# Matrix products of two widths in one kernel: in turn, or sixteen of one and then sixteen of the other

## The chip, the cores and the metric

The kernel runs on one core of a Trainium2 chip. The metric is the device time of one execution in microseconds (us); lower is better. Every number below is from one core.

## What is computed

One layer of a hybrid encoder block on 256 positions of 2048 channels, all in float32:

```
u    = rmsnorm(h) * g1
proj = u @ w_in                      # 2048 -> 1024 + 3 * 1024
y_f  = fourier_mix(proj[:, :1024])   # 2-D DFT per channel group, then a linear map
y_a  = dilated_attention(q, k, v)    # 8 heads of 128, three (window, dilation) pairs, ALiBi
h    = h + concat(y_f, y_a) @ w_out  # 2048 -> 2048
u    = rmsnorm(h) * g2
h    = h + relu(u @ w_up) ** 2 @ w_down   # 2048 -> 8192 -> 2048
out  = rmsnorm(h) * g3
```

The weights are some 190 MB, read once; nearly all of the arithmetic is in the products with `w_in`, `w_out`, `w_up` and `w_down`.

## The kernel before

**Two parts per number.** TensorE multiplies a shortened float32 (`F32R`). Every operand x is therefore split into `hi`, its shortened form, which ScalarE writes (line 130), and `lo` = x - hi, which VectorE writes (line 131). A product of two operands is the sum hi·hi + hi·lo + lo·hi, gathered in PSUM.

**Chunks.** The weights come in 1 MB chunks of 128 x 2048 in an order fixed by `_order`. `load_next` has SyncE fetch a chunk into `w_raw`, ScalarE cast it to `w_hi` and VectorE subtract to `w_lo`, the last two in two halves of 1024 columns each. Each of the three tiles has three buffers, and `chunk` keeps two chunks loaded ahead. So the cast of a chunk waits until the products that read the buffer's former `w_hi`, three chunks earlier, are done, and the subtraction waits for those that read the former `w_lo`.

**Strips** (`strip`) make an output of 256 x 512: the activations are the stationary operand, and 512 columns of weights stream. A chunk gives 2 x 4 x 3 = 24 products of 512 columns (`mm3`, lines 138 to 140), and a strip has four chunks: 96 products. `w_out`, `w_down` and the Fourier and v parts of `w_in` are done so.

**Columns** (`column`) make an output of 128 channels x 256 positions, already transposed for what follows: the weights are the stationary operand, and the activations stream. A row of the tile `u` holds the 256 columns of u_hi and then the 256 of u_lo. For each of the 16 slices of 128 channels of the input there is

- a **wide** product (line 237): w_hi against all 512 columns, into all of the PSUM tile `acc`;
- a **narrow** product (line 238): w_lo against the 256 columns of u_hi, added to the second half of `acc`.

`total` (lines 245, 246) then adds the two halves: ScalarE copies one out of PSUM (its COPY), VectorE adds the other. There are 80 columns: 16 for q and k of the eight heads, and 4 x 16 for `w_up`, each group of 16 followed by the four strips of its `w_down` part. (The first column of the MLP takes its own way through `need`.)

**Work in between.** `later` keeps a list of generators and `part` advances each by a step. A column calls `part` after its products 7 and 15. The heads use this: the scores q·k (narrow products into an `aux` tile), a softmax on VectorE and ScalarE, four transposes of the probabilities (line 476), the products with v (narrow too), each a set number of parts after the former. The instruction streams of the engines are made by a scheduler from this program and are executed in order on each engine.

Lines named below: 130 and 131 the split, 138 to 140 `mm3`, 237 and 238 the column, 245 and 246 `total`, 444 the scaling of q and k, 476 the transposes.

Of the kernel before, what the change touches and what calls it, by code (L numbers as in the profile page):

```python
# [20 lines left out]
KT = D // P  # L21
# [11 lines left out]
FIRST = (4, 4, 2, 2, 2)  # L33
WARM = 9
FEW = 224


def _order():
# [30 lines left out]
def tile_block(ctx: ExitStack, tc: tile.TileContext, gx_t, x, w_all, w_f, g_fin,  # L69
# [9 lines left out]
    def acc():  # L79
        return ps_acc.tile([P, NS], F32, name="acc")  # L80
# [18 lines left out]

    few = const.tile([P, FEW], F32, name="few")  # L100
    few_at = [0]

    def small(n, *shape):
        at = few_at[0]
        few_at[0] += n
        assert few_at[0] <= FEW
        t = few[:, at:at + n]
# [70 lines left out]
    def chunk():  # L178
        i = at[0]
        at[0] += 1  # L180
        while len(loaded) < min(i + 1 + AHEAD, len(order)):
            load_next()
        t = loaded[i]
        loaded[i] = None
        return t
# [8 lines left out]
    def part():  # L194
        for gen in list(queue):
            if next(gen, queue) is queue:
                queue.remove(gen)

    def finish():
        while queue:  # L200
            part()
# [23 lines left out]
                part()  # L225
        return ps

    def column(r, parts=(KT // 2 - 1, KT - 1), need=None):

        ps = acc()
        hi, lo = chunk()
        for kt in range(KT):
            if kt == need:
                finish()
            nc.tensor.matmul(ps, hi[:, kt, :], r[:, kt, :], start=kt == 0, stop=False)  # L237
            nc.tensor.matmul(ps[:, S:], lo[:, kt, :], r[:, kt, :S], start=False, stop=kt == KT - 1)  # L238
            if kt in parts:
                part()  # L240
        return ps[:, :S], ps[:, S:]

    def total(ps, pool):
# [244 lines left out]
    for a in range(2):  # L488
        if a:
            ps_v = strip(u_hi, u_lo)  # L490
        v = values(ps_v)
        for hd in range(a * 4, a * 4 + 4):
            q = channels(column(u), "qt", inv_q)
            k = channels(column(u), "kt", inv_k)
            later(head(hd, q, k, v, (2, 3, 2) if hd < NH - 1 else (2, 3, 1)))
# [53 lines left out]
    for gi in range(NGRP):  # L549
        pool = acts if gi % 2 else mlp  # L550
        hidden = [pool.tile([P, KT, S], F32R, name=f"y_{s}") for s in ("hi", "lo")]
        for j in range(KT):
            if gi == 0 and j == 0:
                ps = column(u2, parts=(4, 6, 8), need=KT - CK)
                inv2 = inverse(sums(ss2, "n2"), "n2")
                nc.vector.tensor_copy(out=inv_u, in_=across(inv2, lambda: mlp.tile([P, S], F32, name="relu", bufs=2)[:, :P]))
            else:
                ps = column(u2)
            up(ps, hidden, j)
        for n in range(NN):  # L560
            final = gi == NGRP - 1
            if final and n == NN - 1:
                break
            ps = strip(*hidden)
            ns = slice(n * NS, (n + 1) * NS)
            for m in range(NM):
                hs = h[m][:, ns]
                nc.vector.tensor_add(out=hs, in0=hs, in1=ps[m])  # L568
                if final:
                    squares(ss3, m, n)  # L570
                    nc.vector.tensor_mul(out=hs, in0=hs, in1=g_b[:, ns])
# [121 lines left out]
```

## Time and profile before

| | |
|---|---|
| three runs | 1030.74, 1031.51, 1031.53 us (median 1031.51) |
| the profiled execution | 1031.32 us |
| its span, first to last instruction | 1029.5 us |
| mean granted TensorE clock | 0.999 of full speed |
| TensorE busy (its matmuls) | 1020.2 us, 99% |
| VectorE, ScalarE busy | 610.0 us (59%), 502.8 us (49%) |
| DMA | 195.10 MB, mean 189 GB/s |

The profile names engines PE (TensorE's products), PEld (its loads of the stationary operand, each before its product, beside the product that runs), DVE (VectorE), ACT (ScalarE) and SP (SyncE). The duration given for a product is longer than the distance from its start to the next one's start, because products overlap in the pipeline; so what a product costs is read from the distances between starts, not from the durations or from the busy share.

### The profile page before, as it was taken

The page shows a single profiled execution, that of the slowest core. Times are in us where ns is not written, and L with a number is a line of the kernel's source. Part 1 is how long each engine was busy: PE and PEld are TensorE (multiplying, and loading weights), DVE is VectorE, ACT ScalarE, POOL GpSimd, SP SyncE. Part 2 cuts the span into 40 slices and gives each one's busy share as a digit, 9 for nine tenths or more (in the row PEclk, how much of TensorE's full clock was granted, in tenths as well). Part 3 has the DMA queues.
Part 4 walks back from the last instruction along what each step waited for, and adds up shares of the span by engine and source line. Part 5 has one row for each costly group of instructions (what it writes and reads, how often), then busy time and mean ns, then how long its engine had stood idle before and what let it go on. Part 6 is the DMA issues. An engine that isn't in the chain of part 4 may idle for free.

```text
span 1029.5 us, 12994 instructions
## 1 busy us (share of the span) xinstructions
PE 1020.2 (99%) x5254; PEld 868.3 (84%) x5254; DVE 610.0 (59%) x846; ACT 502.8 (49%) x741; POOL 1.3 (0%) x10
## 2 busy tenths in 40 slices
PE   9999999999999999999999999999999999999997
PEld 7888888888888888888888888888888888888886
DVE  6975775775456656445656545556554546565553
ACT  7754554554446555333555533355543335554441
POOL 0000000000000000000000000000000000000000
PEclk9999999999999999999999999999999999999999
DMA  8653645444555555555554555555555555555542
GB/s 320 233 225 115 263 169 192 156 180 164 189 220 184 184 193 177 202 199 179 195 185 183 202 180 191 204 178 190 187 183 203 198 180 195 180 189 201 180 152 82
DMA packets 32683, 195.10 MB, mean 189 GB/s; under 512 B 3568, under 2 KB 6128, under 8 KB 10608
## 3 DMA queue, kind: packets, MB, share of 16 engines
q1 hardware_dynamic: 32624, 194.28, 53.1%
q8 instruction: 41, 0.67, 0.2%
q14 instruction: 18, 0.15, 0.0%
HBM read 192.17 MB, written 2.10 MB: 189 GB/s over the span
## 4 chain that ended last, share of the span: by engine, by line
PE 97%; DMA 1%; SPq 0%; DVE 0%; ACT 0%; issue 0%; ACTq 0%
PE acc L237 29%; PE acc L139 16%; PE acc L140 16%; PE acc L138 16%; PE acc L238 15%; PE aux L138 1%; PE aux L140 1%; PE aux L139 1%; DMA w_raw<-w_all 1%; SPq L92 0%; PE aux L521 0%; PE aux L476 0%; DVE w_lo L131 0%; ACT w_hi L130 0%; ACT gh L616 0%
## 5 line engine op out<-in xcount | busy, mean ns | idle before, releaser
L131 DVE TENSOR_TENSOR w_lo<-w_raw,w_hi 128x1024 fp32r<-128x1024 f32 (+1 forms) x356 | 423.7, 1209 | 283.2 <-ACT w_hi L130 283.0
L130 ACT CAST w_hi<-w_raw 128x1024 fp32r<-128x1024 f32 (+1 forms) x356 | 362.1, 1041 | 312.6 <-PE acc L140 223.8
L237 PE MATMUL acc<-u,w_hi 128*128 128x512 f32 x1280 | 453.7, 399 | 0.0
L238 PE MATMUL acc<-u,w_lo 128*128 128x256 f32 x1280 | 359.6, 281 | 0.0
L237 PEld LDWEIGHTS acc<-u,w_hi 128*128 128x128 f32 x1280 | 240.6, 188 | 59.0
L138 PE MATMUL acc<-w_hi,y_hi 128*128 128x512 f32 x624 | 243.7, 391 | 0.0
L140 PE MATMUL acc<-w_hi,y_lo 128*128 128x512 f32 x624 | 242.9, 389 | 0.0
L139 PE MATMUL acc<-w_lo,y_hi 128*128 128x512 f32 x624 | 242.9, 389 | 0.0
L238 PEld LDWEIGHTS acc<-u,w_lo 128*128 128x128 f32 x1280 | 241.8, 189 | 0.2
L140 PEld LDWEIGHTS acc<-w_hi,y_lo 128*128 128x128 f32 x624 | 117.1, 188 | 24.6
L138 PEld LDWEIGHTS acc<-w_hi,y_hi 128*128 128x128 f32 x624 | 117.1, 188 | 24.1
L139 PEld LDWEIGHTS acc<-w_lo,y_hi 128*128 128x128 f32 x624 | 117.2, 188 | 23.7
L545 ACT ACTIVATE sq<-relu 128x256 f32<-128x256 f32 x64 | 26.7, 418 | 118.8 <-DVE relu L543 118.8
L131 DVE TENSOR_TENSOR y_lo<-sq,y_hi 128x256 fp32r<-128x256 f32 x64 | 27.2, 425 | 58.0 <-ACT y_hi L130 58.0
L139 PE MATMUL acc<-w_lo,u 128*128 128x512 f32 x120 | 47.2, 394 | 0.5 <-DVE w_lo L131 0.5
L140 PE MATMUL acc<-w_hi,u 128*128 128x512 f32 x120 | 46.8, 390 | 0.0
L138 PE MATMUL acc<-w_hi,u 128*128 128x512 f32 x120 | 46.6, 395 | 0.1
L246 DVE TENSOR_TENSOR total<-acc,total 128x256 f32<-128x256 f32 x80 | 33.4, 418 | 2.6 <-ACT total L245 2.6
L245 ACT COPY total<-acc 128x256 f32<-128x256 f32 x80 | 29.3, 366 | 8.0 <-PE acc L238 8.0
L568 DVE TENSOR_TENSOR gh<-gh,acc 128x512 f32<-128x512 f32 x30 | 20.5, 684 | 16.8 <-PE acc L140 16.8
L139 PEld LDWEIGHTS acc<-w_lo,u 128*128 128x128 f32 x120 | 22.6, 188 | 5.6 <-DVE w_lo L131 1.6
L130 ACT CAST y_hi<-sq 128x256 fp32r<-128x256 f32 x64 | 26.0, 406 | 2.0
(141 smaller groups left out, 474.3 us busy)
## 6 DMA issues: line engine op xcount, KB each, us to landing
w_raw<-w_all SPq DMA_DIRECT2D x171, 1024.0 KB, 4.7
w_raw<-w_all SPq DMA_DIRECT2D x6, 512.0 KB, 7.8
w_raw<-w_all SPq DMA_DIRECT2D x8, 256.0 KB, 5.0
gh<-x SPq DMA_DIRECT2D x8, 256.0 KB, 6.4
out<-gh SPq DMA_DIRECT2D x6, 256.0 KB, 2.4
gh<-gx_t SPq DMA_DIRECT2D x4, 256.0 KB, 6.1
wf<-w_f SPq DMA_DIRECT2D x4, 256.0 KB, 5.0
g_b<-g_fin SPq DMA_DIRECT2D x1, 1024.0 KB, 4.6
```

The costliest lines, as they stand in the source:

```text
L130: nc.scalar.copy(out=hi, in_=src)
L131: nc.vector.tensor_tensor(out=lo, in0=src, in1=f32(hi), op=ALU.subtract)
L138: nc.tensor.matmul(ps, l_hi, r_hi, start=first, stop=False)
L139: nc.tensor.matmul(ps, l_hi, r_lo, start=False, stop=False)
L140: nc.tensor.matmul(ps, l_lo, r_hi, start=False, stop=last)
L237: nc.tensor.matmul(ps, hi[:, kt, :], r[:, kt, :], start=kt == 0, stop=False)
L238: nc.tensor.matmul(ps[:, S:], lo[:, kt, :], r[:, kt, :S], start=False, stop=kt == KT - 1)
L245: nc.scalar.copy(out=t, in_=ps[1])
L246: nc.vector.tensor_tensor(out=t, in0=ps[0], in1=t, op=ALU.add)
L545: nc.scalar.activation(q, r, AF.Square)
L568: nc.vector.tensor_add(out=hs, in0=hs, in1=ps[m])
```

## The change

All but one of the 80 columns now issue the 16 wide products first and then the 16 narrow ones. The products, their operands and their destinations are the same. The first call of `part` in a column moves from behind the eighth pair to behind the twelfth wide product, the second stays at the end. The column with `need` keeps the old order.

```
-    def column(r, parts=(KT // 2 - 1, KT - 1), need=None):
+    def column(r, parts=None, need=None):
         ps = acc()
         hi, lo = chunk()
-        for kt in range(KT):
-            if kt == need:
-                finish()
+
+        def large(kt):
             nc.tensor.matmul(ps, hi[:, kt, :], r[:, kt, :], start=kt == 0, stop=False)
+
+        def few_columns(kt):
             nc.tensor.matmul(ps[:, S:], lo[:, kt, :], r[:, kt, :S], start=False, stop=kt == KT - 1)
-            if kt in parts:
-                part()
+
+        if need is not None:
+            for kt in range(KT):
+                if kt == need:
+                    finish()
+                large(kt)
+                few_columns(kt)
+                if kt in parts:
+                    part()
+        else:
+            for kt in range(KT):
+                large(kt)
+                if kt == MIDDLE:
+                    part()
+            for kt in range(KT):
+                few_columns(kt)
+            part()
         return ps[:, :S], ps[:, S:]
```

`MIDDLE` is 11. Three places show what the scheduler makes of it. The lines of the changed kernel are shifted: 237 and 240 are its wide and narrow product, 131 and 132 its split, 262 and 263 its `total`, 461 its scaling, 493 its transposes.

TensorE in the second half of the heads: a column for k (acc_1824) in which the transposes of an earlier head's probabilities (s1_1755) are placed. Before:

```order
L237 MATMUL acc_1824<-u_89,w_hi_1709 128x512
L238 MATMUL acc_1824<-u_89,w_lo_1710 128x256
L476 MATMUL aux_1849<-ident_70,s1_1755 128x128 x4
L237 MATMUL acc_1824<-u_89,w_hi_1709 128x512
L238 MATMUL acc_1824<-u_89,w_lo_1710 128x256
```

and now, from the column ahead of it to the next head's scores:

```order
L237 MATMUL acc_1775<-u_89,w_hi_1660 128x512 x16
L240 MATMUL acc_1775<-u_89,w_lo_1661 128x256 x16
L237 MATMUL acc_1824<-u_89,w_hi_1709 128x512 x12
L493 MATMUL aux_1845<-ident_70,s1_1755 128x128 x4
L237 MATMUL acc_1824<-u_89,w_hi_1709 128x512 x4
L240 MATMUL acc_1824<-u_89,w_lo_1710 128x256 x16
L139 MATMUL aux_1874<-kt_hi_1820,qt_hi_1771 128x256
```

The pairs have become unbroken runs, up to 16 long; the transposes stood between the eighth and the ninth pair and now stand inside the wide run, behind its twelfth product.

ScalarE in the first `w_up` group, around the copy of the sum of column acc_3193; w_hi_3245 is the chunk whose buffer that column frees. Before:

```order
L130 CAST y_hi_2753<-sq_3189 128x256
L130 CAST w_hi_3245<-w_raw_3244 128x1024
L245 COPY total_3235<-acc_3193 128x256
L130 CAST w_hi_3245<-w_raw_3244 128x1024
L545 ACTIVATE sq_3239<-relu_3234 128x256
```

and now:

```order
L131 CAST y_hi_2753<-sq_3189 128x256
L131 CAST w_hi_3245<-w_raw_3244 128x1024 x2
L262 COPY total_3235<-acc_3193 128x256
L562 ACTIVATE sq_3239<-relu_3234 128x256
L131 CAST y_hi_2753<-sq_3239 128x256
```

Both halves of the cast now stand ahead of the copy; before, one stood on each side of it.

VectorE in the second half of the heads, between the sum of a k column (acc_1775) and the scores that use kt_lo. Before:

```order
L246 TENSOR_TENSOR total_1816<-acc_1775,total_1816 128x256
L131 TENSOR_TENSOR w_lo_1827<-w_raw_1825,w_hi_1826 128x1024
L444 TENSOR_TENSOR total_1816<-total_1816,inv_k_93 128x256
L131 TENSOR_TENSOR p_lo_1855<-aux_1849,p_hi_1854 128x512
L131 TENSOR_TENSOR kt_lo_1821<-total_1816,kt_hi_1820 128x256
```

and now:

```order
L263 TENSOR_TENSOR total_1816<-acc_1775,total_1816 128x256
L132 TENSOR_TENSOR w_lo_1827<-w_raw_1825,w_hi_1826 128x1024
L461 TENSOR_TENSOR total_1816<-total_1816,inv_k_93 128x256
L132 TENSOR_TENSOR kt_lo_1821<-total_1816,kt_hi_1820 128x256
L132 TENSOR_TENSOR p_lo_1851<-aux_1845,p_hi_1850 128x512
```

kt_lo, for which the next scores wait, has moved ahead of the split of the probabilities. The order of SyncE's transfers is the same in both kernels.

## Rows read from the trace of the kernel before

**Rows 1.** Page, parts 1 and 2: TensorE's busy time; granted clock in 40 slices

```profile
PE 1020.2 (99%) x5254; PEld 868.3 (84%) x5254; DVE 610.0 (59%) x846; ACT 502.8 (49%) x741; POOL 1.3 (0%) x10
...
PEclk9999999999999999999999999999999999999999
```

**Rows 2.** Page, part 4: the chain that ended last, shares by engine, by line

```profile
PE 97%; DMA 1%; SPq 0%; DVE 0%; ACT 0%; issue 0%; ACTq 0%
PE acc L237 29%; PE acc L139 16%; PE acc L140 16%; PE acc L138 16%; PE acc L238 15%; PE aux L138 1%; PE aux L140 1%; PE aux L139 1%; DMA w_raw<-w_all 1%; SPq L92 0%; PE aux L521 0%; PE aux L476 0%; DVE w_lo L131 0%; ACT w_hi L130 0%; ACT gh L616 0%
```

**Rows 3.** Windows, TensorE: 16 columns; 4 strips; 12 narrow, 12 wide, 12 narrow

```profile
core 0: us, PE busy (x), PEclk, DMA share, GB/s
488.56:579.00 90.44, 90.44 (x514) 1.00 0.53 186
579.00:666.07 87.07, 87.07 (x387) 1.00 0.55 193
86.92:88.35 1.43, 1.43 (x13) 1.00 0.00 0
88.35:91.10 2.75, 2.75 (x14) 1.00 0.03 6
91.10:92.53 1.43, 1.43 (x13) 1.00 0.00 0
```

**Rows 4.** Timeline, TensorE (start, duration): column block's start, strips' first product, next block

```profile
488.56 0.39 PE L237 MATMUL acc<-u,w_hi 128*128 128x512 f32 x1
488.79 0.28 PE L238 MATMUL acc<-u,w_lo 128*128 128x256 f32 x1
488.90 0.40 PE L237 MATMUL acc<-u,w_hi 128*128 128x512 f32 x1
489.13 0.28 PE L238 MATMUL acc<-u,w_lo 128*128 128x256 f32 x1
489.25 0.40 PE L237 MATMUL acc<-u,w_hi 128*128 128x512 f32 x1
489.49 0.28 PE L238 MATMUL acc<-u,w_lo 128*128 128x256 f32 x1
...
579.00 0.40 PE L138 MATMUL acc<-w_hi,y_hi 128*128 128x512 f32 x1
...
666.07 0.39 PE L237 MATMUL acc<-u,w_hi 128*128 128x512 f32 x1
```

**Rows 5.** Timeline, TensorE, Fourier stage: 12 narrow, 12 wide, 12 narrow in runs

```profile
86.92 0.28 PE L138 MATMUL aux<-a_hi,f_hi 128*128 128x256 f32 x1
...
88.35 0.40 PE L138 MATMUL acc<-w_hi,u 128*128 128x512 f32 x1
88.58 0.40 PE L139 MATMUL acc<-w_lo,u 128*128 128x512 f32 x1
...
91.10 0.28 PE L138 MATMUL aux<-a_hi,f_hi 128*128 128x256 f32 x1
...
92.53 0.40 PE L237 MATMUL acc<-u,w_hi 128*128 128x512 f32 x1
```

**Rows 6.** Timeline, TensorE, the tail: 24 narrow products, first, and what follows

```profile
1002.04 0.28 PE L138 MATMUL aux<-w_hi,y_hi 128*128 128x256 f32 x1
...
1004.91 0.40 PE L138 MATMUL acc<-w_hi,y_hi 128*128 128x512 f32 x1
```

**Rows 7.** Groups by line: busy us, mean ns of one, idle before: a narrow product's load

```profile
L238 PEld LDWEIGHTS acc<-u,w_lo 128*128 128x128 f32 x1280 | 241.8, 189 | 0.2
```

**Rows 8.** Timeline, ScalarE, around a column's end at 344.97 us

```profile
345.05 1.05 ACT L130 CAST w_hi<-w_raw 128x1024 fp32r<-128x1024 f32 x1 [0.65 <-PE acc L237]
346.01 0.36 ACT L245 COPY total<-acc 128x256 f32<-128x256 f32 x1
```

**Rows 9.** Timeline: VectorE's kt_lo of a head, and TensorE's scores that read it

```profile
183.15 0.42 DVE L131 TENSOR_TENSOR kt_lo<-total,kt_hi 128x256 fp32r<-128x256 f32 x1 [0.47 <-ACT kt_hi L130]
...
184.10 0.28 PE L138 MATMUL aux<-kt_hi,qt_hi 128*128 128x256 f32 x1
```

More of the change, by code (lines that the diff above doesn't have):

```diff
@@ L35 @@
 FEW = 224
+MIDDLE = 11
 def _order():
```

## The prediction, made before the changed kernel had run

> **What bounds the kernel now.** I read the page's busy shares first, then the chain of waits, then the starts of the products. TensorE is busy 99% of the span, and the clock row is at full speed in all 40 slices [rows 1]; the chain that ended last is 97% TensorE, with lines 237 and 238, the column's two products, at 29% and 15% of the span [rows 2]. So the time is the sum of the distances between starts on TensorE, and VectorE, ScalarE and the transfers matter only where they would make it wait. A busy share of 99% does not say that TensorE goes as fast as it can: the durations in the timeline (0.40 and 0.28 us) are longer than the distances, because products overlap. The distances tell more.
>
> In a block of 16 columns, 488.56 to 579.00 us, there are 256 pairs of a wide and a narrow product in 90.44 us: **353.3 ns a pair**, 5.653 us a column (the view's x514 counts two products that reach in from before; the program has 512) [rows 3, 4]. Inside, the wide product takes 0.23 to 0.24 us and the narrow one 0.11 to 0.12 [rows 4].
>
> In the four strips after it, 579.00 to 666.07 us, there are only wide products, 4 x 96 = 384 in 87.07 us: **226.7 ns each** [rows 3, 4]. In the tail 24 narrow products stand in a row, 1002.04 to 1004.91: 2.87 us, **119.6 ns each** [rows 6]. A wide and a narrow one, each among its own kind, thus make 346.3 ns, against 353.3 in turn. The same widths cost 7.0 ns more per pair when they alternate. That is what the change can get at.
>
> **The hand-over.** A run must also be left. The Fourier stage has the pattern that the change would make, only shorter: 12 narrow, 12 wide, 12 narrow, without a break [rows 5]. The 12 wide take 2.75 us, 229.2 ns each, not 226.7; the 12 narrow take 1.43 us, 119.2 ns each [rows 3, 5]. From 88.35 to 92.53 a whole turn of 12 + 12 takes 4.18 us, where 12 x 346.3 ns would be 4.156: a turn costs 0.024 us beyond the pure rates, paid by the first wide products behind a narrow run (88.35 to 88.58 is 0.23). A column in the new order has one such turn.
>
> **The sum.**
> - New column: 4.18 us for 12 + 12, and four more of each at the rates of the long runs, 4 x 0.2267 + 4 x 0.1196 = 1.385, gives 5.565 us. Old column: 5.653. Difference 0.088 us.
> - Columns changed: 80 less the one with `need` = 79. 79 x 0.088 = 6.9 us.
> - Groups that now split a wide run. Behind the twelfth wide product stand the transposes of a head (they stood between pairs before; their own cost is the same) or six narrow products with v, and once the first head's scores stand inside a run. Some seven such places get a turn of their own: 7 x 0.024 = 0.2 us back. The other scores stand behind a narrow run and only lengthen it.
> - Products, loads, bytes and splits are unchanged in number: nothing. SyncE's order is unchanged, and the transfers are busy 0.53 of the time in the columns [rows 3]; a column shorter by 1.6% makes that 0.54: nothing.
>
> Together **6.7 us**. Off the profiled execution's 1031.32 us that leaves 1024.6; the median of the three runs lies 0.2 above that execution, so **1024.8 us**.
>
> **What the moved instructions could do to TensorE.** The last wide product of a column now ends 16 x 0.12 = 1.9 us before the column does, so ScalarE's cast for the next chunk but one, which waits for it (the wait is named in the row: PE acc L237), can begin 1.9 us earlier [rows 8]. Both halves, 2 x 1.05 us, now stand before the copy of the column's sum and end some 0.1 us after the column; in the trace the copy came at 346.01, 1.04 us after the column's end at 344.97, behind one half cast [rows 8]. So the copy comes about 0.9 us earlier, and with it everything made of the sum. The subtraction for w_lo waits now for the last narrow product, that is for the column's end; before, it waited for the half cast that stood ahead of the copy, which ended later than that (345.05 + 1.05) [rows 8], so nothing is later for it. The narrowest margin that I found is a head's kt_lo, ready at 183.57 (183.15 + 0.42), for scores that start at 184.10: 0.53 us [rows 9]. It hangs on the copy, so it grows by most of 0.9 us, less the 0.1 us by which the column between is shorter; kt_lo's place on VectorE has moved forward too. The transposes come 12 x 0.2267 = 2.7 us into their column instead of 8 x 0.3533 = 2.8: 0.1 us earlier, and the column before it is 0.1 shorter, a small loss of margin. I cost all this at nothing; if that cover were gone, each head would lose what its chain is late, a few tenths of a us, some 2 us over eight heads.
>
> **Bounds of the unknown.** Runs of 16 with the tile `u` streaming and fresh weights stand nowhere in the trace. On the good side the turn costs nothing: 16 x 346.3 = 5.541 us a column, 79 x 0.112 = 8.8 us, 1022.7. On the bad side the wide ones stay at the Fourier run's mean of 229.2 throughout and the narrow ones at 119.6: 16 x 348.8 = 5.581, 79 x 0.072 = 5.7 us, 1025.8. I take the built-up column, because the strips show that 226.7 is reached again in long runs. With the 2 us of the heads and a little more the upper end is 1028.
>
> **Rivals.**
> 1. *Each product has its price whatever stands beside it* (9%). Then the 7 ns are not of the alternation but of something that columns have and strips have not, for instance `u` as the streaming operand with weights as the stationary one. For it: no column in the trace has another order. Against it: the first wide product of the block, which follows a wide one of a strip, took 0.23 us (488.56 to 488.79), and a strip's wide product behind a narrow one took 0.23 to 0.24 as in columns [rows 4, 5]. It gives 1031.5 us, no change. The Trainium skill, page "TensorE: Matmul & The Clock Gate", section "Back-to-back issue gap", has such a rule: a gap of N/2.4 + 2.5 ns for N columns, which would be 216 and 109 ns, 325 a pair in either order. The trace disagrees with its sizes: 353.3 a pair, and less than that where widths are in runs.
> 2. *A long narrow run is held by its weight loads* (4%, ends slower). In turn, the load for a narrow product goes beside a wide one; in a run of 16 each load has only a narrow product to hide behind. The profile gives a load 189 ns [rows 7]. If loads could not overlap each other, a narrow product would cost 189 ns instead of 120, 79 x 16 x 69 ns = 87 us, about 1112 us in all. The change turns into a loss as soon as a narrow product in a run costs 6.7 us / 1264 = 5.3 ns more than 119.6, that is from 125 ns. Against it: the 24 narrow products of the tail have a load each and run at 119.6. The same page's section "LDWEIGHTS (loading the stationary operand)" gives a load as columns / 1.2, 107 ns for 128 columns; that just fits under a narrow product, and the row of 119.6 ns agrees with it as a floor.
> 3. *The turn is free* (13%): 1022.7, as above. Against it stands the one turn measured.
> 4. *The heads' chains are late* (8%): TensorE waits some tenths of a us for kt_lo or the probabilities; 1027 or so, still faster.
>
> That the change does not do what it says is excluded: the built streams show the runs of 16.
>
> **The numbers.** The forecast of 1024.8 has 66%. Rivals 3 and 4 lie on the same side, so faster has 0.87; rival 1 is no change, 0.09; rival 2 slower, 0.04. A measurement of this kernel can tell about 0.2%, 2.1 us, from no change; the forecast is 0.65% off. The range takes in the free turn with a little to spare and the late heads: 1022.5 to 1028.0. It leaves out rivals 1 and 2.
>
> **What would show it.** In the changed kernel's timeline, wide products inside a column at 0.227 us from start to start with the first five or so slower, narrow ones at 0.120; a block of 16 columns in 16 x 5.565 = 89.0 us instead of 90.44, and the strips unchanged at 87.1. ScalarE's copy of the sum should follow the column's end by some 0.2 us instead of 1.04. Wrong it would be if wide products stayed at 0.236 in their runs (rival 1), if narrow ones stood at 0.125 or above (rival 2), if a turn showed no slow products (rival 3), or if TensorE had waits on kt_lo or on the transposes' input (rival 4).

## The result, and the profile after

The changed kernel took **1023.88 us** in the median of six runs (1023.22 to 1024.13), beside 1031.52 for the kernel before in six runs of the same comparison (1030.74 to 1032.36). The ratio is 0.993, with a 95% interval of 0.992 to 0.994: 7.6 us faster. Forecast were 1024.8 us and a range of 1022.5 to 1028.0.

The page of the changed kernel, parts 1 and 4 (those of before are [rows 1, 2]):

```profile
PE 1012.7 (99%) x5254; PEld 869.2 (85%) x5254; DVE 610.7 (60%) x846; ACT 496.3 (49%) x741; POOL 1.3 (0%) x10
...
PE 97%; DMA 1%; SPq 0%; DVE 0%; ACT 0%; issue 0%; ACTq 0%
```

The same number of products and loads, the same 99%, the same 97% of the chain: in shares nothing has happened. TensorE was busy all the time before and is so now, in 7 us less. The place of the gain shows in the windows (us, TensorE busy, granted clock, DMA share, GB/s) of a block of 16 columns and of the four strips behind it, which answer to [rows 3]:

```profile
485.51:574.55 89.04, 89.04 (x513) 1.00 0.54 192
574.55:661.62 87.07, 87.07 (x387) 1.00 0.55 191
```

The strips still take 87.07 us, to the last digit. The block of columns takes 89.04 instead of 90.44. Inside, the timeline (start, duration; equal products merged) shows the runs:

```profile
491.05 3.82 PE L237 MATMUL acc<-u,w_hi 128*128 128x512 f32 x16
494.70 2.08 PE L240 MATMUL acc<-u,w_lo 128*128 128x256 f32 x16
496.62 3.82 PE L237 MATMUL acc<-u,w_hi 128*128 128x512 f32 x16
500.27 2.08 PE L240 MATMUL acc<-u,w_lo 128*128 128x256 f32 x16
502.18 1.09 PE L237 MATMUL acc<-u,w_hi 128*128 128x512 f32 x4
```

From start to start a wide run takes 3.65 us, 228 ns a product, and a narrow one 1.91 to 1.92, 120 ns a product. 16 times the 226.7 ns of the strips would be 3.627: the wide run bears 0.02 us for the turn.

Split at the first column, the profiled executions read as follows, before:

```profile
0.00:92.53 92.53, 90.86 (x468) 1.00 0.59 216
92.53:1029.50 936.97, 929.36 (x4788) 1.00 0.53 187
```

and after:

```profile
0.00:92.04 92.04, 90.09 (x469) 1.00 0.59 218
92.04:1022.30 930.26, 922.60 (x4788) 1.00 0.53 188
```

From the first column on the change gives 936.97 - 930.26 = **6.71 us**. Another 0.49 us of the two spans' difference lies ahead of the first column, where the program is the same; the second profile of the changed kernel (below) shows how far the start varies by itself.

### The profile page after: what moved, and what is told of

It reads as the page before. It is cut to its first block, busy times and chain, and to the rows that moved or that the text cites. A ratio compares the mean times of both kernels' runs of the same rounds, so it can differ in the third digit from the quotient of the medians.

```text
span 1022.3 us, 13002 instructions
## 1 busy us (share of the span) xinstructions
PE 1012.7 (99%) x5254; PEld 869.2 (85%) x5254; DVE 610.7 (60%) x846; ACT 496.3 (49%) x741; POOL 1.3 (0%) x10
## 4 chain that ended last, share of the span: by engine, by line
PE 97%; DMA 1%; SPq 0%; DVE 0%; ACT 0%; issue 0%; ACTq 0%
PE acc L237 29%; PE acc L140 16%; PE acc L141 16%; PE acc L139 16%; PE acc L240 15%; PE aux L139 1%; PE aux L141 1%; PE aux L140 1%; DMA w_raw<-w_all 1%; SPq L93 0%; PE aux L538 0%; PE aux L493 0%; DVE w_lo L132 0%; ACT w_hi L131 0%; ACT gh L633 0%
## 5 line engine op out<-in xcount | busy, mean ns | idle before, releaser
L131 ACT CAST w_hi<-w_raw 128x1024 fp32r<-128x1024 f32 (+1 forms) x356 | 354.1, 1038 | 251.5 <-PE acc L141 228.2
L237 PE MATMUL acc<-u,w_hi 128*128 128x512 f32 x1280 | 309.5, 391 | 0.0
L237 PEld LDWEIGHTS acc<-u,w_hi 128*128 128x128 f32 x1280 | 234.8, 188 | 45.1
L240 PEld LDWEIGHTS acc<-u,w_lo 128*128 128x128 f32 x1280 | 165.1, 191 | 6.2
L240 PE MATMUL acc<-u,w_lo 128*128 128x256 f32 x1280 | 168.4, 283 | 0.0
L141 PEld LDWEIGHTS acc<-w_hi,y_lo 128*128 128x128 f32 x624 | 117.2, 188 | 24.6
L140 PEld LDWEIGHTS acc<-w_lo,y_hi 128*128 128x128 f32 x624 | 117.2, 188 | 23.8
L139 PEld LDWEIGHTS acc<-w_hi,y_hi 128*128 128x128 f32 x624 | 117.2, 188 | 23.7
L140 PEld LDWEIGHTS acc<-w_lo,u 128*128 128x128 f32 x120 | 22.6, 188 | 5.2 <-DVE w_lo L132 1.1
```

The source lines that it names most:

```text
L131: nc.scalar.copy(out=hi, in_=src)
L139: nc.tensor.matmul(ps, l_hi, r_hi, start=first, stop=False)
L140: nc.tensor.matmul(ps, l_hi, r_lo, start=False, stop=False)
L141: nc.tensor.matmul(ps, l_lo, r_hi, start=False, stop=last)
```

## The experiments

**Is it the order of the widths, or the work that moved with it?** One kernel keeps the old order and takes only the new place of the first `part`:

```
+            for kt in range(KT):
+                large(kt)
+                few_columns(kt)
+                if kt in (MIDDLE, KT - 1):
+                    part()
```

> The old order, wide and narrow in turn, but with the first call of part behind the twelfth pair, so that only the place of the work in between is the change's. Theory (the gain is of runs against turns of width): a block of 16 columns stays at 90.44 us and the time at 1031.5 us, within 0.6. Rival (the gain came from the work in between or from what ScalarE does earlier): some of the 7.6 us appears here, 1024 to 1029.

Measured: 1030.51 us beside 1030.96 for the kernel before, ratio 0.9994 (0.9984 to 1.0004), no difference. Its block of columns:

```profile
487.72:578.16 90.44, 90.44 (x514) 1.00 0.53 187
```

The place of the work in between is worth nothing; the gain is of the order of the products.

**Is it the width, or the weights and the destination that alternate too?** In the old order three things alternate: 512 and 256 columns, w_hi and w_lo, the whole tile and its second half. This kernel makes nearly all products narrow and lets the other two alternate:

```
+            large(0)
+            few_columns(0)
+            for kt in range(1, KT):
+                nc.tensor.matmul(ps[:, :S], hi[:, kt, :], r[:, kt, :S], start=False, stop=False)
+                nc.tensor.matmul(ps[:, S:], hi[:, kt, :], r[:, kt, S:], start=False, stop=False)
+                few_columns(kt)
```

> Every wide product but a column's first is cut into two of 256 columns with the same weights, so that nearly all have one width, while the weights still alternate between hi and lo and the destination between the two halves of the tile. Theory (the extra is paid for a turn of width alone): 46 x 0.120 + 0.227 + some 0.01 = 5.76 us a column, a block of 92.1 us, (5.76 - 5.565) x 79 = 15 us over the changed kernel, 1039 us. Rival (the 7 ns of a pair come from alternating hi and lo weights or from alternating the destination): 7 ns on each of some 30 to 46 products more, 0.2 to 0.3 us a column, 1055 to 1064 us.

Measured: 1039.44 us, beside 1030.96. Its block, and the starts inside a column (254: first half, 255: second half with w_hi, 240: second half with w_lo):

```profile
491.34:583.38 92.04, 92.04 (x754) 1.00 0.53 184
```

```profile
499.83 0.28 PE L240 MATMUL acc<-u,w_lo 128*128 128x256 f32 x1
499.95 0.28 PE L254 MATMUL acc<-u,w_hi 128*128 128x256 f32 x1
500.07 0.29 PE L255 MATMUL acc<-u,w_hi 128*128 128x256 f32 x1
500.19 0.28 PE L240 MATMUL acc<-u,w_lo 128*128 128x256 f32 x1
```

5.753 us a column, less one wide product of 0.227, leaves 5.526 for 46 narrow ones: 120.1 ns, the rate of an unbroken run, although from each product to the next the weights, the destination or both change. So neither of these costs anything where all products have one width, and the extra cost goes with the alternation of the widths. (Whether any change of width has a price is looked at below.)

**How long must a run be?** The same kernel with runs of 4, of 2 and of 8 (`n`):

```
-            for kt in range(KT):
-                large(kt)
-                if kt == MIDDLE:
-                    part()
-            for kt in range(KT):
-                few_columns(kt)
+            for k0 in range(0, KT, n):
+                for kt in range(k0, k0 + n):
+                    large(kt)
+                    if kt == MIDDLE:
+                        part()
+                for kt in range(k0, k0 + n):
+                    few_columns(kt)
             part()
```

Runs of 4:

> Runs of 4 wide and 4 narrow, four turns a column instead of one. Theory (a turn has a price that builds up over some five wide products): the first four wide behind a narrow run took 233 + 236 + 228 + 233 in the changed kernel, 23 ns over the pure rate, the first two narrow 7.5 ns under it, so a turn costs some 16 ns; 4 x 16 over 5.547 us is 5.61 us a column, a block of 89.8 us, 1028 us in all. Rival A (any turn costs the full 18 ns of a long one): 5.62 us a column, 89.9 us, hardly told apart by the time, but the starts tell. Rival B (16 in a row are needed, the price is one per product that has another neighbour): 1030 or more. Rival C (a run of four is as good as one of sixteen): 1024.

Measured: 1027.3 us beside 1030.96, ratio 0.9965 (0.9952 to 0.9978); the block:

```profile
485.63:575.42 89.79, 89.79 (x513) 1.00 0.54 188
```

As the theory said, 89.8 and 1028; rivals B and C fell. Rival A, some 0.1 us a block higher, is too near to be told apart by the time; from the starts a turn costs 17 ns here (table below). Then runs of 2:

> Runs of 2 wide and 2 narrow, eight turns a column. Theory (the price of a turn builds up over the wide products behind it: 6.6 ns if one follows, 16 if four do, 18 if sixteen do): 10 to 13 ns a turn, 5.547 + 8 x 0.0115 = 5.64 us a column, a block of 90.0 to 90.4, 1029.5 to 1031 us: a run of two gains next to nothing. Rival (the price is one per product with another neighbour, halved by runs of two): half the gain of the full runs, a block of 89.7, 1027.5 us.

Measured: 1024.48 us beside 1030.56, ratio 0.9937 (0.9919 to 0.9955). A clear miss of both: runs of two are nearly as good as runs of sixteen. The block, and the chain that ended last (start, us, what) inside a column:

```profile
485.24:574.41 89.17, 89.17 (x514) 1.00 0.55 189
```

```profile
520.00 0.23 PE acc L240 x2
520.23 0.46 PE acc L237 x2
520.69 0.23 PE acc L240 x2
520.92 0.47 PE acc L237 x2
```

Two wide take 0.46 to 0.47, two narrow 0.23, where the undisturbed rates would make 0.453 and 0.240. So a turn has two sides: wide products behind narrow ones lose, narrow ones behind wide ones gain, and with two of each the sides nearly cancel. The forecast let the sum of the two grow steadily with the length. With each side by itself, the runs of 8 were forecast:

> Runs of 8 wide and 8 narrow, two turns a column. After the runs of two, the price of a turn is taken as a sum of two: what the wide products behind a narrow run lose (about 10, 13, 23, 27 ns for 1, 2, 4, 16 of them), less what the narrow ones behind a wide run gain (about 3, 10, 8, 8 ns). Theory: with eight both are complete, 27 - 8 = 19 ns a turn, 5.547 + 2 x 0.019 = 5.585 us a column, a block of 89.36 us, between the runs of sixteen (89.04) and those of four (89.79), 1025 us. Rival (the price depends on the length in no such order, as the runs of two made it look): a block under 89.1 or over 89.6.

Measured: 1025.82 us beside 1031.31, ratio 0.9945 (0.9923 to 0.9968), and the block as expected:

```profile
486.06:575.42 89.36, 89.36 (x513) 1.00 0.55 193
```

**Two columns in one**, 32 wide and then 32 narrow products, which needs both chunks at hand (the chunk after them is loaded between the two narrow runs):

```
+        for ps, hi in ((pa, ha), (pb, hb)):
+            for kt in range(KT):
+                nc.tensor.matmul(ps, hi[:, kt, :], r[:, kt, :], start=kt == 0, stop=False)
...
+        for ps, lo in ((pa, la), (pb, lb)):
+            for kt in range(KT):
+                nc.tensor.matmul(ps[:, S:], lo[:, kt, :], r[:, kt, :S], start=False, stop=kt == KT - 1)
```

> Two columns together: 32 wide products, then 32 narrow ones, half the turns. Theory: 16 x 5.547 + 8 x 0.018 = 88.9 us a block instead of 89.04, some 0.7 us less in all, 1023.2 us; wide products at 227 ns in the run but for the first five, narrow at 120. Rival (the two sums that end close together make VectorE or ScalarE late for TensorE): waits in the attention columns or gaps between columns, 1024 to 1028.

Measured: 1023.39 us beside 1030.96, ratio 0.9927 (0.9912 to 0.9942). TensorE has no wait behind the start in its trace, so the rival fell. Once more, with the changed kernel itself on the same chip:

> The changed kernel once more, beside the one with two columns together on the same chip, for the small difference between them. Theory (only the distances inside the columns differ): about 1023.4 us where the kernel before is at 1031; the sum of the column blocks 455.4 us again, and whatever the time differs from 1023.9 lies outside the columns, mainly ahead of the first one. Rival (the 0.9 us beyond the forecast belongs to the change): the start of the first column block is again 0.5 us earlier than in the kernel before of the same call.

> Two columns together, again. Theory: the column blocks sum to 454.7 us, 0.7 us less than in the changed kernel, and the time is 0.7 us less, about 0.07%, at the edge of what five rounds can tell. Rival (the saved turns come back as waits elsewhere): no difference between the two.

Measured: the changed kernel 1023.68, ratio 0.9933 (0.9921 to 0.9945); two columns together 1023.41, ratio 0.9928 (0.9914 to 0.9941). The block of two columns together is shorter, as forecast, in its first profile:

```profile
485.28:574.16 88.88, 88.88 (x513) 1.00 0.53 188
```

0.16 us a block, some 0.8 us over 80 columns, lies within the intervals of the two ratios, so by time the two kernels can't be told apart. (The second profile has 88.88 us too.) It is the fastest that was run, by an amount that only the trace shows.

The changed kernel's second profiled execution took 1025.23 us, the first 1024.08. Its windows, split at the first column:

```profile
0.00:93.18 93.18, 90.83 (x469) 1.00 0.60 215
93.18:1023.40 930.22, 922.60 (x4788) 1.00 0.54 188
```

930.22 against 930.26: from the first column on the same. The whole difference, 1.14 us, lies ahead of it. So the start of the same kernel varies by more than the 0.49 us by which the first profile was better there than the kernel before, and the rival that gave them to the change fell: here the start, 93.18, is later than the 92.53 of the one profile of the kernel before. (That one is of an earlier comparison; of the kernel before there is no profile beside this one.)

The lengths together. The undisturbed rates, 226.7 ns for a wide product and 120.0 for a narrow one inside a run, make 256 x 346.7 = 88.76 us a block; what a block has beyond it is divided by its turns. The last columns are means over the starts in the block's trace: what the wide products of a run lose, and the narrow ones gain, against these rates (226.67 and 120.0 ns).

| run | block, us | turns in a block | beyond, per turn | wide lose | narrow gain | a turn inside the block |
|---|---|---|---|---|---|---|
| 1 (before) | 90.44 | 256 | 6.6 ns | 9.4 | 2.8 | 6.6 ns |
| 2 | 89.17 | 128 | 3.2 ns | 13.0 | 9.6 | 3.4 ns |
| 4 | 89.79 | 64 | 16 ns | 22.6 | 6.0 | 17 ns |
| 8 | 89.36 | 32 | 19 ns | 27.5 | 7.5 | 20 ns |
| 16 (the change) | 89.04 | 16 | 18 ns | 27.5 | 7.5 | 20 ns |
| 32 | 88.88 | 8 | 15 ns | 27.6 | 7.6 | 20 ns |

That "beyond, per turn" falls from 8 to 32 comes from the block's edge (and from the rounded rates): its first wide run stands behind the strips, behind no narrow run, and loses nothing, 3.63 us against the 3.65 of the next one:

```profile
485.51 3.79 PE L237 MATMUL acc<-u,w_hi 128*128 128x512 f32 x16
489.14 2.08 PE L240 MATMUL acc<-u,w_lo 128*128 128x256 f32 x16
```

Inside the block a turn costs the same 20 ns from runs of eight on. In the changed kernel the first five wide products behind a narrow run stand 233, 236, 228, 232 and 231 ns apart and all further ones 226.7; the first two narrow ones 113 and 119, all further ones 120.0. A run of eight holds both stretches whole; the shorter ones cut them off.

**How near was the loss by the weight loads?** The second rival of the prediction. Each narrow product is cut into two of 128 columns, each with its own load:

```
+            for c in range(0, S, P):
+                nc.tensor.matmul(ps[:, S + c:S + c + P], lo[:, kt, :], r[:, kt, c:c + P], start=False,
+                                 stop=kt == KT - 1 and c == P)
```

> Every narrow product is cut into two of 128 columns with the same weights, each with its own load, in the new order (16 wide, then 32 of 128). It asks how near a narrow product of 256 columns is to being held by its weight load. Theory (a load needs about as long as three of the transposes took from start to start, 109 ns, and a product can not follow faster): 32 x 0.109 instead of 16 x 0.120 us, 1.57 us more a column, 79 columns 124 us more, about 1148 us. Rival (the price goes by the streamed columns alone, as 226.7 for 512 and 120 for 256 suggest, so some 67 ns for 128): 32 x 0.067 = 2.14, 0.22 us more a column, 1041 us.

Measured: 1159.74 us beside 1030.56. The timeline:

```profile
550.57 3.68 PE L241 MATMUL acc<-u,w_lo 128*128 128x128 f32 x32
554.09 3.90 PE L237 MATMUL acc<-u,w_hi 128*128 128x512 f32 x16
557.83 3.68 PE L241 MATMUL acc<-u,w_lo 128*128 128x128 f32 x32
```

32 products of 128 columns take 3.52 us, 110 ns each, and the wide run behind them 3.74 instead of 3.65; put to their account that makes 113 ns. Half the columns cost hardly less than the 120 ns of 256. That there is a floor was right, its height, 109 forecast, a little low, and the time 12 us over the 1148 expected. That the loads set it is the theory's reading: no run leaves a load out. By it, a product of 256 columns stands only 7 to 10 ns above what the loads allow. The Trainium skill, page "TensorE: Matmul & The Clock Gate", section "LDWEIGHTS (loading the stationary operand)", gives a load as columns / 1.2, which is 107 ns for 128 columns; the measured 110 to 113 ns are slightly above that.

**Is the price of a turn due to that nearness?** If so it should vanish when the narrow product is well above the floor. Two kernels stream 384 columns in place of 256, one in runs, one in turn:

```
-            nc.tensor.matmul(ps[:, S:], lo[:, kt, :], r[:, kt, :S], start=False, stop=kt == KT - 1)
+            nc.tensor.matmul(ps[:, P:], lo[:, kt, :], r[:, kt, P:], start=False, stop=kt == KT - 1)
```

> The narrow products of the 79 columns stream 384 columns (128 to 511 of the row of u, into the same columns of the tile) instead of 256, in runs of sixteen. They leave out w_lo's product with the first 128 positions of u_hi and add its product with u_lo, so this run computes something else; only its distances are read. By a straight line between 120 ns for 256 and 226.7 for 512 a product of 384 takes 173.3 ns, and a column 16 x 400.0 = 6.401 us, a block of 102.4 us without any price for turns. Theory (the price of a turn arises because a product of 256 columns, 120 ns, is close to the 112 ns that a load needs by the run with products of 128): no price, a block of 102.4. Rival (any turn of width costs it): 16 x 0.018 to 0.024 more, 102.7 to 102.8.

> The same products of 512 and 384 columns, in turn (with the part calls of the run that had only these moved); it leaves out and adds the same terms. Theory (the load is the cause): no price either, a block of 102.4 us, the same as in runs. Rival (any turn of width costs it): 6.6 ns a pair as in the kernel before, 256 x 6.6 = 1.7 us more, 104.1.

Measured, one execution each: 1095.68 us in runs, 1102.31 in turn. The block in runs, and in turn:

```profile
513.60:617.03 103.43, 103.43 (x514) 1.00 0.49 169
```

```profile
518.30:622.40 104.10, 104.10 (x514) 1.00 0.47 165
```

In turn the block is 1.7 us over the 102.4 of the undisturbed rates, 6.6 ns a pair, the same sum as for 512 and 256 columns in turn. The theory fell: 384 columns are far above the floor and pay the same. The rival had this number right, but not that of the runs: there a turn costs (103.43 - 102.4) / 16 = 64 ns, three times what it costs beside 256. The timeline of the runs shows where:

```profile
543.10 2.96 PE L240 MATMUL acc<-u,w_lo 128*128 128x384 f32 x16
545.90 3.83 PE L237 MATMUL acc<-u,w_hi 128*128 128x512 f32 x16
549.56 2.96 PE L240 MATMUL acc<-u,w_lo 128*128 128x384 f32 x16
```

A narrow run takes 2.80 us from start to start, where 16 x 173.3 ns make 2.773, and a wide one 3.66 instead of 3.627. The last ten narrow starts of a run are 173.3 ns apart, so the straight line for 384 columns holds; what is lost is lost in the first six narrow and the first nine wide products. So here both widths lose, and in turn as well (231.7 and 174.9 ns in the mean over the block), whereas beside 256 columns the narrow ones gain (236.1 and 117.2 in the kernel before). The equal 6.6 ns are made of different parts.

**Does every change of width have a price?** No. In one strip of the changed kernel, six narrow products of the scores and later six with v stand between wide ones. Of the timeline, three products are shown for each: the first narrow one, and the first and the fifth wide one behind the six. For the scores:

```profile
147.02 0.28 PE L139 MATMUL aux<-kt_hi,qt_hi 128*128 128x256 f32 x1
...
147.73 0.40 PE L139 MATMUL acc<-w_hi,u 128*128 128x512 f32 x1
...
148.66 0.39 PE L140 MATMUL acc<-w_lo,u 128*128 128x512 f32 x1
```

and for the products with v:

```profile
150.48 0.28 PE L139 MATMUL aux<-p_hi,v_hi 128*128 128x256 f32 x1
...
151.19 0.39 PE L139 MATMUL acc<-w_hi,u 128*128 128x512 f32 x1
...
152.09 0.39 PE L140 MATMUL acc<-w_lo,u 128*128 128x512 f32 x1
```

Behind the scores four wide products take 0.93 us, 23 ns over the undisturbed rate; behind the products with v they take 0.90 to 0.91, the undisturbed rate from the first one on. This is so at all eight places where six products with v stand by themselves between wide ones, and in all eight again in the second profile of the changed kernel; and there the six take 706 or 707 ns, 13 less than 6 x 120. So the price of the columns goes with the alternation of their two widths, but a change of width alone doesn't make it: the same widths change there for nothing. What sets the products with v apart was not tested. Nor was a kernel run in which a product has no load of its own (5254 products, 5254 loads), so the loads may have a part in it. Why the price is as high as it is, why it is lost on one side and gained on the other, and why two in a row nearly cancel, stays open too.

## Why the prediction was right

- **The bound.** Right. TensorE's starts set the time before and after; the strips did not move (87.07 us in both).
- **The rates and the turn.** Right: 5.565 us forecast for a column, 89.04 / 16 = 5.565 measured. The stretch of 12 narrow, 12 wide and 12 narrow products in the Fourier stage [rows 5] was the change on a small scale, and its 4.18 us could be carried over: within 1 ns its distances are those of the changed kernel, the slow first five wide ones included. The first rival is ruled out by the shorter block; the kernel in which only `part` moved excludes the other explanation by the work in between. One reading was off without harm: the prediction laid the turn's 24 ns on the wide products alone, beside 119.6 ns for a narrow one. Measured, the wide lose 27.5 and the first two narrow gain 7.5 against 120.0; the 119.6 of the tail already held that gain, and the sum is the same.
- **The choice of the stretch** was partly luck. The trace of the kernel before also has turns without a price: behind the four sixes of products with v that stand by themselves in a strip, the wide ones run at 226.7 ns at once. The prediction did not see them and had "the one turn measured" against its third rival. Other turns of that trace have the price (the Fourier stage's, the scores', the tail's), but why the columns should go like these the prediction did not say, and no run shows it. Had they gone the other way, with nothing lost on the wide side and 13 ns gained on the narrow one, a column would have taken 16 x 346.7 ns less 13, 5.534 us, and the time some 1022 us, an estimate that lies just below the range.
- **The count.** Right: 79 columns and a few split runs made 6.7 us, and 6.71 were found from the first column on. The three full blocks give 1.40 us each, 0.0875 a column. The 31 columns ahead of them, with what lies between, give 2.57 (308.98 against 306.41 us), where 31 x 0.0875 would be 2.71, so the split runs took back some 0.14 us, forecast 0.2. There are ten such places, not seven: five with transposes, one with scores, and four with products with v, behind which the wide ones lose nothing. The other 0.9 us between the forecast 1024.8 and the median 1023.88 are not of the change: half a microsecond is the spread of the start, and the medians of the kernel before lay between 1030.56 and 1031.52.
- **The second rival**, weight loads, did not come, but its mechanism was near: a narrow product would have had to cost 125 ns, it costs 120, and the floor found with products of 128 columns is 110 to 113. At 128 columns the loss is there.
- **The third**, a free turn, is excluded: a wide run still takes 3.65 us, not 3.627, and 32 in a row are better than 16 by as much as half the turns are worth.
- **The fourth**, late heads, did not come. TensorE's waits in the changed kernel (total us, times, longest) all lie ahead of the first column:

```profile
PE aux L115 <- DVE ones L98: 1.0, 1, 1.0
PE acc L140 <- DVE w_lo L132: 0.5, 1, 0.5
PE acc L139 <- ACT w_hi L131: 0.3, 1, 0.3
```

The narrowest margin found grew as reckoned, from 0.53 us [rows 9] to 182.66 - 181.28 = 1.38 (first column start, second duration; kt_lo of VectorE, the scores of TensorE):

```profile
180.85 0.43 DVE L132 TENSOR_TENSOR kt_lo<-total,kt_hi 128x256 fp32r<-128x256 f32 x1 [0.47 <-ACT kt_hi L131]
```

```profile
182.66 0.28 PE L139 MATMUL aux<-kt_hi,qt_hi 128*128 128x256 f32 x1
```

One detail was off. The copy of a column's sum was to follow the column's end by 0.2 us; it follows by 0.41, 343.19 for a column that ends at 342.78:

```profile
340.98 0.41 ACT L131 CAST y_hi<-sq 128x256 fp32r<-128x256 f32 x1
341.29 1.99 ACT L131 CAST w_hi<-w_raw 128x1024 fp32r<-128x1024 f32 x2
343.19 0.36 ACT L262 COPY total<-acc 128x256 f32<-128x256 f32 x1
```

In this `w_up` group the casts, 2 us now in one piece ahead of the copy, begin not with the last wide product but behind y_hi of the column before. The copy is still 0.6 us earlier than in the kernel before [rows 8], and nobody on the path waits for it. In the heads, where no y_hi stands there, it came as forecast: at 182.91 us, 0.25 behind the column that ends at 182.66.

## What to carry to other kernels

An engine that is 99% busy can still be slowed by the order of its work: compare the distance from start to start of the same instruction in stages that mix and stages that don't, and look in the trace for a stretch that already has the order you want. Look for all such stretches: here two kinds of them disagreed, and which one the new order would follow had to be measured. Sorting the columns' products of two widths into runs was worth some 0.7% of this kernel; but the length is to be measured, since runs of four were worse than runs of two. Cutting the narrow products to 128 columns, each with its own load, cost 136 us (1159.74 beside 1023.68 us for the changed kernel in the same comparison).

## What had not been expected of the hardware

- The price of a turn between 512 and 256 columns does not grow steadily with the length of the run: inside the columns' block it is 6.6, 3.4 and 17 ns for runs of 1, 2 and 4, and 20 ns for 8, 16 and 32 alike. Runs of two, 1024.48 beside 1030.56 us, already give 6.1 us.
- Not every change of width has that price: six products of 256 columns with v, between wide ones, take 706 or 707 ns, and the wide ones behind them 226.7 each at once.
- It does not depend on a narrow product being near the floor of 110 to 113 ns: 384 columns beside 512 pay 6.6 ns a pair in turn, as 256 do, and 64 ns a turn in runs of sixteen.
- The undisturbed distances inside long runs, 120 ns for 256 columns, 173.3 for 384 and 226.7 for 512, lie on N / 2.4 + 13.3 ns. The Trainium skill, page "TensorE: Matmul & The Clock Gate", section "Back-to-back issue gap", has N / 2.4 + 2.5 for the gap of an isolated product: the trace agrees in the slope and not in the fixed part, for products that each bring a load.
